# Silu in one ScalarE step, and the place of the MLP norm's sums of squares

## The chip, the cores and the metric

The kernel runs on one core of a Trainium2 chip. The time is the device time of one execution in microseconds; a comparison uses the median of several executions. The engines are named as the profile names them: PE is the matrix engine (PEld its weight loads), DVE the vector engine, ACT the scalar engine, POOL GpSimd, SP the queue that issues nearly all DMAs. Each engine works through its own list of instructions in order; semaphores tie the lists together.

## The reference

Two decoder layers over 512 tokens and 1024 features, in fp32. Cut to what the change touches:

```python
z = h @ w_in                       # split into attention q k v, retention q k v g, two gates
r = chunkwise_retention(rq, rk, rv)
r = r * lax.rsqrt(jnp.mean(r * r, axis=-1, keepdims=True) + EPS)
r = r.reshape(B, S, RET_V) * jax.nn.silu(rg.astype(jnp.float32))
...
h2 = rmsnorm(x, g_mlp)
x = x + jnp.square(jax.nn.relu(h2 @ w_up)) @ w_down
```

`rg` has 1024 columns, eight chunks of 128. `rmsnorm` divides each token by the root of the mean of its squares.

## The kernel before

Activations lie feature-major: eight chunks of 128 features by 512 tokens. Every fp32 factor is split into a high and a low part in a reduced format, and a product is three matmuls, high by high, high by low, low by high (`products`, L332 to L334). Weights arrive in units of 128 x 1024 (SP's DMAs into `raw`); ACT rounds a unit to its high half (L286) and DVE subtracts for the low half (L287). `raw`, `hi` and `lo` have three buffers each, taken in turn, and `unit` splits up to two units ahead of the one in use, so the high half of a unit goes into the buffer of the unit three before.

A layer runs through `w_in` (with attention and retention put between its matmuls as background steps), `w_a`, `w_b`, `w_out` and the MLP. Parts of `w_b`, `w_out` and `w_up` are done as pairs of chunks by a scheme with seven half-size products instead of eight (`narrow_pair` with 256-wide matmuls, `wide_pair` with 512-wide ones for the high weights). A pair uses four pieces of weights and three PSUM banks, called a, b and e. Its first product goes into a, ACT copies a into b (L640), the second product goes into e, and the third adds to b. Later ACT copies the finished b and e into SBUF (L643, L647).

The gates of retention: `put_rg` multiplies a chunk by the token factor on DVE (L970), and `silu` (L976) makes Sigmoid on ACT (L978) and the product with it on DVE (L979). The first four chunks get it after the attention, near the Sigmoid of the other gates (L1124); the last four as they come, while the second half of the retention and the chunks of gate b (`gate`, L904, Sigmoid) run. ACT holds one table of functions at a time; a step whose function is not in the table is preceded by a table load.

The MLP norm: `Rms.prepare` splits the sum over the chunks of x squared into two parts, sh and sl; `Rms.finish` calls `inverse_rms_halved` (L457): two matmuls with a matrix of ones (ssq), two square roots on ACT (L465), a reciprocal on DVE (L466), and four copies on ACT (L469) that lay out rstd. The norm is applied after the matmul, when the products leave PSUM: `put_up` (L1313) for the first four chunks of the MLP, `positive` for the pair behind them. These first four chunks are one `group` (L387): four PSUM banks at once, four units of weights, each unit with two halves (j = 0, 1) of twelve matmuls. A hook after unit 0 calls `prepare`, a hook after unit 1 calls `finish`. Then come the pairs (0, 2), narrow, and (0, 3), wide; the evacuations of the four chunks are put between the steps of the pair.

What sets the order: the program is traced once, in the order of the Python code, and the framework's scheduler then orders each engine's list by its own estimate of times (`schedule_with_timeline_sim=True`). A later call can therefore come earlier in an engine's list. `tc.issue_after(ins)` pins what is traced inside it behind `ins` on the engine of `ins`.

Of the kernel before, what the change touches and what calls it, by code (L numbers as in the profile page):

```python
# [2 lines left out]

# [10 lines left out]
AF = mybir.ActivationFunctionType  # L14
ALU = mybir.AluOpType
# [3 lines left out]
P = 128  # L19
T = 512  # L20
D = 1024
KD = D // P
# [59 lines left out]
def mlp_sequence():  # L82

    seq = [("first", 0, 0), ("pair", 0, 2), ("pair", 0, 3)]
    for q in range(3):
        for i in range(4):
            seq += [("down", q, i), ("pair", q + 1, i)]
    return seq + [("last", 3, 0)]  # L90
# [37 lines left out]
def decoder(ctx, tc, xT, x_first, w_in, w_a, w_b, w_out, w_up, w_down, tables, decay, band, triangles, g_last, out):  # L128
    nc = tc.nc
# [13 lines left out]
    def temp(name="t"):  # L143
        return tmp.tile([P, T], F32, tag="t", name=name)

    def big(name, dtype=F32):
        return tmp.tile([P, 2, T], dtype, tag="big", name=name, bufs=7)

    def bank(pool, name):
        return pool.tile([P, T], F32, tag=pool.name, name=name)  # L150
# [141 lines left out]
    def unit(name, layer):  # L292
        i = state["next"]
        assert order[i][:2] == (layer, name), (order[i], layer, name)
        state["next"] += 1
        split_until(i + 3)
        return parts.pop(i)
# [7 lines left out]
    ones = const.tile([P, P], F32R, name="ones")  # L305
# [20 lines left out]
    def products(ps, pairs, start, stop, resume=False):  # L326


        n = len(pairs)
        for i, ((ah, al), (bh, bl)) in enumerate(pairs):  # L330
            more = {"skip_group_check": True} if resume else {}
            nc.tensor.matmul(ps, ah, bh, start=start and i == 0, stop=False, **more)  # L332
            nc.tensor.matmul(ps, ah, bl, start=False, stop=False, **more)  # L333
            nc.tensor.matmul(ps, al, bh, start=False, stop=stop and i == n - 1, **more)  # L334

    def split(hi, lo, src, scale=None):

        if scale is None:
            nc.scalar.activation(hi, src, AF.Copy)  # L339
            nc.vector.tensor_tensor(lo, src, f32(hi), ALU.subtract)  # L340
        else:
            nc.scalar.activation(hi, src, AF.Copy, scale=scale)  # L342
            nc.vector.scalar_tensor_tensor(lo, src, scale, f32(hi), ALU.mult, ALU.subtract)

    xs, x_homes = [], []
# [6 lines left out]
    def old_input():  # L352
        for t in x_homes:
            slots.give(*t[1])
# [29 lines left out]
        products(ps, pairs[n // 2 :], False, True)  # L384
        evacuate(ps)

    def group(name, layer, moving, evacuates, meanwhile=None):  # L387


        banks = [bank(ps_mm, "mm") for _ in range(4)]  # L390
        for u in range(4):
            hi, lo = unit(name, layer)
            for j in range(2):
                k = 2 * u + j
                for c, ps in enumerate(banks):
                    cols = slice(j * T + c * P, j * T + (c + 1) * P)
                    products(ps, [((hi[:, cols], lo[:, cols]), moving[k])], k == 0, k == KD - 1)
            if meanwhile and u in meanwhile:
                meanwhile[u]()
        return [partial(evacuate, ps) for ps, evacuate in zip(banks, evacuates)]  # L400

    def all_of(steps):
        for step in steps:
            step()
# [52 lines left out]
    def inverse_rms_halved(both, n, dest):  # L457

        ps = bank(ps_aux, "ssq")
        for i, part in enumerate(both):  # L460
            nc.tensor.matmul(ps, ones, part, start=i == 0, stop=i == len(both) - 1)
        own = temp("own")[:, : T // 2]
        sides = [(slice(a * P // 2, (a + 1) * P // 2), slice(a * T // 2, (a + 1) * T // 2)) for a in range(2)]
        for rows, cols in sides:
            nc.scalar.activation(own[rows, :], ps[rows, cols], AF.Sqrt, bias=eps[rows, :], scale=1.0 / n)  # L465
        nc.vector.reciprocal(own, own)  # L466
        for rows, cols in sides:
            for there, _ in sides:
                nc.scalar.activation(dest[there, cols], own[rows, :], AF.Copy)  # L469

    def inverse_rms(both, n, dest):

        ps = bank(ps_aux, "ssq")
        for i, part in enumerate(both):
            nc.tensor.matmul(ps, ones, part, start=i == 0, stop=i == len(both) - 1)
        nc.scalar.activation(dest, ps, AF.Sqrt, bias=eps, scale=1.0 / n)
        nc.vector.reciprocal(dest, dest)
# [12 lines left out]
    class Rms:  # L490
# [7 lines left out]

        def finish(self):
            self.value = tmp.tile([P, T], F32, tag="rstd", name="rstd", bufs=2)  # L500
            (inverse_rms if self.folded else inverse_rms_halved)(self.parts, D, self.value)


    def end(layer, uT):
# [76 lines left out]
    def layer_body(layer):  # L581
        g_mix, g_mlp = 2 * layer, 2 * layer + 1
        rms_mix, rms_mlp = Rms(g_mix, True), Rms(g_mlp, False)
# [10 lines left out]
        def sum_input(by_form, b, ks):  # L594

            (b11, b12), (b21, b22) = ((t[:, :, :H], t[:, :, H:]) for t in b)
            f = [big("sums").rearrange("p a (b t) -> p (a b) t", t=H) for _ in range(2)]
            t1, t2, t3, t4 = f[0][:, 0:2, :], f[0][:, 2:4, :], f[1][:, 0:2, :], f[1][:, 2:4, :]

            def parts_of_forms(j):  # L600
                t = by_form[2 * (j // 2) + ks // 2]
                return [t[:, :, :, s, :] for s in range(2)]

            nc.vector.tensor_tensor(t1, b12, b11, ALU.subtract)
            nc.vector.tensor_tensor(t2, b22, t1, ALU.subtract)
            split(*parts_of_forms(0), f[0].rearrange("p (j k) t -> p j k t", k=2))
            nc.vector.tensor_tensor(t3, b22, b12, ALU.subtract)
            nc.vector.tensor_tensor(t4, b21, t2, ALU.subtract)
            split(*parts_of_forms(2), f[1].rearrange("p (j k) t -> p j k t", k=2))

        def scaled_pair(ks, which):

            b = [big("xg") for _ in range(2)]
            for part, g in ((0, ks), (1, ks + 4)):
                for i in range(2):
                    col = which * KD + g + i
                    nc.scalar.activation(b[part][:, i, :], x[:, g + i, :], AF.Copy, scale=gain[:, col : col + 1])
            return b
# [342 lines left out]
        rg, rg_next, rg_tiles = {}, {}, {}  # L961
# [12 lines left out]
            return put  # L974

        def silu(i):  # L976
            s = temp("sig")
            nc.scalar.activation(s, rg[i], AF.Sigmoid)  # L978
            nc.vector.tensor_tensor(rg[i], rg[i], s, ALU.mult)  # L979

        ret = {}

# [156 lines left out]
        for u in range(4):  # L1139
            hi, lo = unit("w_a", layer)  # L1140
            for j in range(2):
                c = 2 * u + j
                ps = bank(ps_mm, "mm")
                pairs = []
                for k in range(4):
                    cols = slice(k * 256 + j * P, k * 256 + (j + 1) * P)
# [158 lines left out]
        by_form = [h[1] for h in homes_x]  # L1305
# [108 lines left out]
        def put_down(c, last=False):  # L1414
            def put(ps):
                nc.vector.tensor_tensor(x[:, c, :], x[:, c, :], ps, ALU.add)  # L1416
                if last:
                    scaled_input(c, g_mix + 2)
                    squared_input(c, g_mix + 2)
                    nc.sync.dma_start(spill[:, c, :], x[:, c, :])  # L1420

            return put

        def first_hooks():
            def at1():
                rms_mlp.finish()
                sum_input(by_form, scaled_pair(2, g_mlp), 2)

            return {0: lambda: (rms_mlp.prepare(), sum_input(by_form, scaled_pair(0, g_mlp), 0)), 1: at1}

        for what, q, i in mlp_sequence():
            if what == "first":
                late = group("w_up", layer, xs, [put_up] * 4, first_hooks())
            elif what == "pair":
                pair(q, i, late)
                if (q, i) == (3, 3):
                    old_input()
                    for t, _ in homes_x:
                        slots.give(*t[1])
            elif what == "down":  # L1440
                two_chunks("w_down", layer, up[q], [put_down(2 * i), put_down(2 * i + 1)])
                if i == 3:
                    slots.give(*up_slots[q])
            elif layer == DEPTH - 1:
                end(layer, up[q])
            else:
                new_input()
                all_of(group("w_down", layer, up[q], [put_down(c, True) for c in range(4)]))
                for c in range(4, KD):
                    chunk("w_down", layer, up[q], put_down(c, True))  # L1450
                slots.give(*up_slots[q])
# [10 lines left out]
    for layer in range(DEPTH):  # L1462
        layer_body(layer)
# [175 lines left out]
```

## Time and profile before

| what | value |
|---|---|
| median of 3 runs | 1472.45 us (1472.3 to 1472.51) |
| profiled execution | 1473.8 us |
| its span, first to last instruction | 1472.0 us |
| granted PE clock | 0.999 |
| PE busy | 1464.8 us (100%), 7466 matmuls |
| DVE busy | 1166.7 us (79%) |
| ACT busy | 810.9 us (55%) |

A row of the timeline reads: start in us from the span's start, duration, engine, line of the kernel, operation, output<-inputs, shape, count; in brackets the idle time of the engine ahead of it and what ended it. A row of the groups reads: line, engine, operation, count, then busy us and mean ns of one, then idle us ahead and what ended it. PE's matmuls overlap, so the distance of two starts, and not the duration, is what a matmul costs.

### The profile page before, as it was taken

The numbers are of one execution on the slowest core, as the hardware profiler recorded it, in microseconds if no ns is written. First come the engines' busy times: TensorE is split into PE (matmuls) and PEld (weight loads), VectorE is DVE, ScalarE is ACT, GpSimd is POOL, SyncE is SP. The second block draws the span as 40 slices with busy tenths as digits, with TensorE's granted clock in tenths as the row PEclk, the third lists the DMA queues.
The fourth block names the chain that finished last, engine by engine and source line by source line (L and its number), as shares of the span: only waits on it lengthen the run. The fifth ranks groups of instructions, "written<-read, shape, count | busy, mean of one in ns | idle before, by whom it ended". The sixth has DMA issues, their size and how long they took to land.

```text
span 1472.0 us, 20220 instructions
## 1 busy us (share of the span) xinstructions
PE 1464.8 (100%) x7466; PEld 1249.6 (85%) x7466; DVE 1166.7 (79%) x1920; ACT 810.9 (55%) x1306; POOL 3.8 (0%) x14
## 2 busy tenths in 40 slices
PE   9999999999999999999999999999999999999998
PEld 7888888888988888888888888888989888888887
DVE  7998878778988787776678986786899877878763
ACT  7656356654684445444455753656547754444553
POOL 0000000000000000000000000000000000000000
PEclk9999999999999999999999999999999999999999
DMA  6422843356443332333543258333654522333241
GB/s 227 127 89 92 300 158 99 102 172 212 126 126 118 101 115 93 104 104 115 165 126 97 86 186 272 104 104 102 207 171 126 154 95 93 114 106 109 90 140 57
DMA packets 71043, 194.45 MB, mean 132 GB/s; under 512 B 8457, under 2 KB 8609, under 8 KB 70945
## 3 DMA queue, kind: packets, MB, share of 16 engines
q1 hardware_dynamic: 70656, 192.65, 40.7%
q8 instruction: 58, 0.95, 0.3%
q10 hardware_dynamic: 288, 0.52, 0.1%
q14 instruction: 41, 0.33, 0.1%
HBM read 171.63 MB, written 18.89 MB: 129 GB/s over the span
## 4 chain that ended last, share of the span: by engine, by line
PE 94%; issue 5%; DMA 1%; DVE 0%; ACT 0%; POOLq 0%; DVEq 0%; SPq 0%
PE mm L334 22%; PE mm L332 22%; PE mm L333 22%; PE mm L1336 11%; PE mm L1337 5%; PE rv L332 2%; PE rv L333 2%; PE rv L334 2%; PE score L842 1%; PE r L332 1%; PE r L334 1%; PE r L333 1%; PE pT L797 0%; PE pv L823 0%; PE pv L824 0%
## 5 line engine op out<-in xcount | busy, mean ns | idle before, releaser
L333 PE MATMUL mm<-r,hi 128*128 128x512 f32 (+1 forms) x1568 | 572.5, 367 | 0.0
L332 PE MATMUL mm<-r,hi 128*128 128x512 f32 (+1 forms) x1568 | 569.7, 367 | 0.6 <-ACT r L342 0.6
L334 PE MATMUL mm<-r,lo 128*128 128x512 f32 (+1 forms) x1568 | 563.9, 367 | 0.2
L286 ACT ACTIVATE hi<-raw 128x1024 fp32r<-128x1024 f32 (+1 forms) x334 | 334.1, 1002 | 386.4 <-PE mm L333 206.8
L287 DVE TENSOR_TENSOR lo<-raw,hi 128x512 fp32r<-128x512 f32 (+1 forms) x335 | 384.7, 1151 | 111.6 <-ACT hi L286 107.9
L334 PEld LDWEIGHTS mm<-r,lo 128*128 128x128 f32 x1568 | 293.7, 188 | 48.7 <-DVE lo L287 1.4
L332 PEld LDWEIGHTS mm<-r,hi 128*128 128x128 f32 x1568 | 293.8, 188 | 47.5 <-ACT r L342 1.4
L333 PEld LDWEIGHTS mm<-r,hi 128*128 128x128 f32 x1568 | 294.3, 188 | 45.9
L1336 PE MATMUL mm<-r,hi 128*128 128x512 f32 x728 | 252.1, 391 | 0.0
L1337 PE MATMUL mm<-r,lo 128*128 128x256 f32 x728 | 200.5, 277 | 0.0
L1336 PEld LDWEIGHTS mm<-r,hi 128*128 128x128 f32 x728 | 136.5, 188 | 28.6
L1337 PEld LDWEIGHTS mm<-r,lo 128*128 128x128 f32 x728 | 136.7, 188 | 3.1 <-DVE lo L287 0.7
L1416 DVE TENSOR_TENSOR x<-x,mm 128x512 f32<-128x512 f32 x56 | 37.8, 686 | 28.9 <-PE mm L334 28.9
L1409 ACT ACTIVATE z<-z 128x512 f32<-128x512 f32 x56 | 32.4, 623 | 48.7 <-DVE z L1389 48.7
L333 PE MATMUL rv<-lo,r 128*128 128x512 f32 x128 | 49.8, 389 | 0.0
L334 PE MATMUL rv<-hi,r 128*128 128x512 f32 x128 | 49.5, 389 | 0.0
L332 PE MATMUL rv<-hi,r 128*128 128x512 f32 x128 | 49.4, 390 | 0.0
L340 DVE TENSOR_TENSOR r<-z,r 128x512 fp32r<-128x512 f32 x64 | 42.9, 686 | 3.0 <-ACT r L339 2.6
L339 ACT ACTIVATE r<-z 128x512 fp32r<-128x512 f32 x64 | 38.4, 619 | 7.9 <-DVE z L1070 7.8
L869 ACT ACTIVATE sm<-sm,st 128x256 f32<-128x256 f32 (+1 forms) x64 | 30.1, 472 | 18.9 <-DVE st L857 18.7
L1389 DVE SCALAR_TENSOR_TENSOR z<-z,rstd 128x512 f32<-128x512 f32 x52 | 35.7, 687 | 0.6
L340 DVE TENSOR_TENSOR r<-sums,r 128x1024 fp32r<-128x1024 f32 x24 | 28.9, 1220 | 0.0
(273 smaller groups left out, 1693.0 us busy)
## 6 DMA issues: line engine op xcount, KB each, us to landing
raw<-w_in_in SPq DMA_DIRECT2D x89, 512.0 KB, 3.7
raw<-w_down_in SPq DMA_DIRECT2D x64, 512.0 KB, 3.6
raw<-w_up_in SPq DMA_DIRECT2D x32, 512.0 KB, 4.0
raw<-w_up_in SPq DMA_DIRECT2D x60, 256.0 KB, 2.9
raw<-w_a_in SPq DMA_DIRECT2D x8, 512.0 KB, 4.8
ahead<-w_b_in SPq DMA_DIRECT2D x8, 512.0 KB, 5.4
park_w_b<-ahead SPq DMA_DIRECT2D x16, 256.0 KB, 5.7
ahead<-w_up_in SPq DMA_DIRECT2D x8, 512.0 KB, 4.9
```

Source lines behind the costliest of these rows:

```text
L286: nc.scalar.activation(hi[:, at], raw[:, at], AF.Copy)
L287: last_low[:] = [nc.vector.tensor_tensor(lo[:, at], raw[:, at], f32(hi[:, at]), ALU.subtract).ins]
L332: nc.tensor.matmul(ps, ah, bh, start=start and i == 0, stop=False, **more)
L333: nc.tensor.matmul(ps, ah, bl, start=False, stop=False, **more)
L334: nc.tensor.matmul(ps, al, bh, start=False, stop=stop and i == n - 1, **more)
L339: nc.scalar.activation(hi, src, AF.Copy)
L340: nc.vector.tensor_tensor(lo, src, f32(hi), ALU.subtract)
L1336: nc.tensor.matmul(both, hi[:, c], m, start=start and k == 0, stop=False, **more)
L1337: nc.tensor.matmul(ps[:, :H], lo[:, c], m[:, 0, :], start=False, stop=k == 3 and start, **more)
L1389: nc.vector.scalar_tensor_tensor(z[:, :, at], z[:, :, at], 0.0, factor, ALU.max, ALU.mult)
L1409: nc.scalar.activation(z[:, i, :], z[:, i, :], AF.Square)
L1416: nc.vector.tensor_tensor(x[:, c, :], x[:, c, :], ps, ALU.add)
```

## The change

`silu` becomes one ACT step with the Silu function, in place. The call of `rms_mlp.finish` leaves the hook after unit 1. `group` gets an argument `between`: ahead of the second half of its last unit it is called, and that half's matmuls are pinned behind the last of the two ssq matmuls on PE. `inverse_rms_halved` and `Rms.finish` return that matmul.

```diff
-    def group(name, layer, moving, evacuates, meanwhile=None):
+    def group(name, layer, moving, evacuates, meanwhile=None, between=None):
...
                 k = 2 * u + j
-                for c, ps in enumerate(banks):
-                    cols = slice(j * T + c * P, j * T + (c + 1) * P)
-                    products(ps, [((hi[:, cols], lo[:, cols]), moving[k])], k == 0, k == KD - 1)
+                with tc.issue_after(between()) if between and (u, j) == (3, 1) else nullcontext():
+                    for c, ps in enumerate(banks):
+                        cols = slice(j * T + c * P, j * T + (c + 1) * P)
+                        products(ps, [((hi[:, cols], lo[:, cols]), moving[k])], k == 0, k == KD - 1)
...
-            nc.tensor.matmul(ps, ones, part, start=i == 0, stop=i == len(both) - 1)
+            summed = nc.tensor.matmul(ps, ones, part, start=i == 0, stop=i == len(both) - 1).ins
...
+        return summed
...
-            (inverse_rms if self.folded else inverse_rms_halved)(self.parts, D, self.value)
+            return (inverse_rms if self.folded else inverse_rms_halved)(self.parts, D, self.value)
...
         def silu(i):
-            s = temp("sig")
-            nc.scalar.activation(s, rg[i], AF.Sigmoid)
-            nc.vector.tensor_tensor(rg[i], rg[i], s, ALU.mult)
+            nc.scalar.activation(rg[i], rg[i], AF.Silu)
...
-            def at1():
-                rms_mlp.finish()
-                sum_input(by_form, scaled_pair(2, g_mlp), 2)
+            def at0():
+                rms_mlp.prepare()
+                sum_input(by_form, scaled_pair(0, g_mlp), 0)
 
-            return {0: lambda: (rms_mlp.prepare(), sum_input(by_form, scaled_pair(0, g_mlp), 0)), 1: at1}
+            return {0: at0, 1: lambda: sum_input(by_form, scaled_pair(2, g_mlp), 2)}
...
-                late = group("w_up", layer, xs, [put_up] * 4, first_hooks())
+                late = group("w_up", layer, xs, [put_up] * 4, first_hooks(), rms_mlp.finish)
```

More of the change, by code (lines that the diff above doesn't have):

```diff
@@ L1 @@
 from contextlib import ExitStack
+from contextlib import nullcontext
 from functools import partial
```

## The prediction

> **What bounds the kernel now.** I read the page first (span, busy time, chain), then the list of who waited for whom on PE and on its weight loads, then the timeline of the two places that the edits touch.
>
> ```profile
> span 1472.0 us, 20220 instructions
> ...
> PE 1464.8 (100%) x7466; PEld 1249.6 (85%) x7466; DVE 1166.7 (79%) x1920; ACT 810.9 (55%) x1306; POOL 3.8 (0%) x14
> ...
> PE 94%; issue 5%; DMA 1%; DVE 0%; ACT 0%; POOLq 0%; DVEq 0%; SPq 0%
> ```
>
> PE is busy from end to end and the chain of work that ended last is nearly all PE. A change that leaves the 7466 matmuls alone can only take away waits of PE, or add some. The list of waits (in all, times, longest) says how much there is to take:
>
> ```profile
> PE warm L311 <- DVE ones L306: 1.0, 1, 1.0
> PEld mm L334 <- DVE lo L287: 1.4, 6, 0.3
> PEld mm L1337 <- DVE lo L287: 0.7, 2, 0.3
> ```
>
> Beside the start-up, PE's weight loads wait for low halves that DVE brings late, 2.1 us in all. That is 0.14% of the span and the most that these edits could win. I count 0.2% (2.94 us) as about what a measurement of this kernel can tell from no change, so a gain beyond it is all but excluded. The question is which new waits arise.
>
> **The sums below** are differences, made against the profiled execution (1473.8 us; its span is 1472.0). The median of the unprofiled runs is 1472.45, 1.35 lower; I add the differences to that median.
>
> **Edit 1, silu in one step.** Per layer eight Sigmoids and eight products leave, eight Silus come. The groups (count, then busy and mean ns of one, then idle before) and two stretches (PE, PEld, DVE, ACT busy us of the stretch) of the gates of layer 0:
>
> ```profile
> L979 DVE TENSOR_TENSOR z<-z,sig 128x512 f32<-128x512 f32 x16 | 10.7, 686 | 3.5 <-ACT sig L978 3.5
> L978 ACT ACTIVATE sig<-z 128x512 f32<-128x512 f32 x16 | 9.6, 622 | 0.1
> L978 ACT ACT_TABLE_LOAD x2 | 2.6, 1283 | 0.2 <-DVE z L970 0.2
> ```
> ```profile
> 120.00:160.00 40.00, 40.00 (x182) 33.12 (x181) 34.67 (x63) 23.87 (x31) 0.00 (x0) 1.00 0.45 143
> 240.00:330.00 90.00, 90.00 (x460) 77.26 (x459) 70.87 (x104) 53.97 (x79) 0.00 (x0) 1.00 0.40 127
> ```
> ```profile
> L286 ACT ACTIVATE hi<-raw 128x1024 fp32r<-128x1024 f32 (+1 forms) x35 | 36.5, 1044 | 43.4 <-PE mm L333 33.1 <-issue 5.3 <-PE rv L334 4.5
> ```
>
> DVE loses 16 x 0.686 = 11.0 us of work. No Silu is in this trace; I price it as the Sigmoid of the same tile, 0.62 us, so ACT's arithmetic stays. Silu is not in Sigmoid's table: the changed program has 23 table loads where this one has 19, two more per layer. One stands ahead of the first four Silus (behind the Sigmoid of the other gates, in the first stretch), one ahead of the Sigmoids that follow the last four (in the second). A load costs what these two rows show, load and next step 1.30 us apart:
>
> ```profile
> 253.90 1.28 ACT L978 ACT_TABLE_LOAD   x1 [0.17 <-DVE z L970]
> 255.20 0.63 ACT L978 ACTIVATE sig<-z 128x512 f32<-128x512 f32 x1
> ```
>
> So ACT gains 4 x 1.30 = 5.2 us and DVE loses 11.0. What does PE see of it? In both stretches PE is busy throughout, so nothing is there to win. ACT is busy 24 of 40 and 54 of 90 us. Its weight splits between 120 and 330 us (the last row of the groups) stood idle for 43.4 us, 33.1 of them because PE had not yet freed the buffer: ACT runs ahead of PE and catches up 1.3 us within one or two units. I take 0 for edit 1; the cover is that head start. Bounds: 0 below, since PE has no idle time here to give back; 5.2 us above, if all four loads fell on PE's path. Zero is nearer, by the 33.1.
>
> The page "ScalarE: Activation LUTs" of the Trainium skill, section "What ACT_TABLE_LOAD costs", speaks against this edit: it asks for about 1.28 us of load plus 1.38 of drain, 2.66 a switch. By it ACT would gain an estimated 10.6 us, still hidden, or 10.6 on the path at worst. The trace has the load but no drain behind it (1.30 from row to row), so the trace decides.
>
> **Edit 2, the squares between the halves.** The "first" group multiplies four chunks in four units (512-wide), then the pair behind it runs in four pieces (256-wide products; I call its banks a, b, e as the code does). Before, the two ssq products stood inside the last unit; PE in layer 0, then ACT, then DVE:
>
> ```profile
> 418.06 0.39 PE L333 MATMUL mm<-r,hi 128*128 128x512 f32 x1
> ...
> 420.77 0.39 PE L461 MATMUL ssq<-sh,ones 128*128 128x512 f32 x1
> 421.00 0.39 PE L333 MATMUL mm<-r,hi 128*128 128x512 f32 x1
> ...
> 423.72 0.39 PE L461 MATMUL ssq<-sl,ones 128*128 128x512 f32 x1
> ...
> 424.40 0.28 PE L332 MATMUL mm<-r,hi 128*128 128x256 f32 x1
> ...
> 425.81 0.28 PE L332 MATMUL mm<-r,hi 128*128 128x256 f32 x1
> ...
> 427.23 0.28 PE L332 MATMUL mm<-r,hi 128*128 128x256 f32 x1
> ```
> ```profile
> 418.53 1.06 ACT L286 ACTIVATE hi<-raw 128x1024 fp32r<-128x1024 f32 x1 [2.01 <-PE mm L333]
> 419.50 1.04 ACT L339 ACTIVATE r<-sums 128x1024 fp32r<-128x1024 f32 x1
> 420.56 1.28 ACT L465 ACT_TABLE_LOAD   x1
> 424.15 0.95 ACT L465 ACTIVATE own<-ssq,x 64x256 f32<-64x256 f32 x2 [2.31 <-PE ssq L461]
> 425.12 1.06 ACT L286 ACTIVATE hi<-raw 128x1024 fp32r<-128x1024 f32 x1
> 426.21 0.37 ACT L640 ACTIVATE mm<-mm 128x256 f32<-128x256 f32 x1
> 426.92 1.70 ACT L469 ACTIVATE rstd<-own 64x256 f32<-64x256 f32 x4 [0.34 <-DVE own L466]
> 428.64 0.63 ACT L286 ACTIVATE hi<-raw 128x512 fp32r<-128x512 f32 x1
> ```
> ```profile
> 419.63 1.23 DVE L287 TENSOR_TENSOR lo<-raw,hi 128x1024 fp32r<-128x1024 f32 x1
> ...
> 425.13 1.75 DVE L466 RECIPROCAL own<-own 128x256 f32<-128x256 f32 x1 [3.14 <-ACT own L465]
> ```
>
> A 512-wide product takes 0.227 us of PE (420.77 to 421.00), a 256-wide one 0.118 (twelve from 424.40 to 425.81). In the changed program PE's order is: the rest of the first half (two products), ssq<-sh, ten of the pair's twelve products into a, ssq<-sl, all twelve products of the second half, the last two into a, then e and b as before. So:
> - ssq<-sh at 420.77 + 2 x 0.227 = 421.22. The ten moved ahead need piece 0's low half at about 421.7; it is there at 419.63 + 1.23 = 420.86. No wait.
> - ssq<-sl at 421.22 + 0.23 + 10 x 0.118 = 422.63, which is 1.09 earlier. ACT's square roots start 0.43 behind it (423.72 to 424.15), at 423.06, and end at 424.01; the reciprocal ends at 424.04 + 1.75 = 425.79.
> - The second half runs from 422.86; its last product with the high weights is the eleventh, at 422.86 + 10 x 0.227 = 425.13. PE's sum of work is the same, so e is due at 425.81 and the next b at 427.23, unchanged.
>
> The catch is ACT's order. Behind the square roots comes, as before, the high half of the pair's piece 2. There are three weight buffers, and this half goes where unit 3, the last of the group, still lies. ACT follows the freeing product by 0.47 us (418.06 to 418.53), so it starts at 425.13 + 0.47 = 425.60, with ACT standing idle from 424.01. Behind it now stand the four rstd copies and only then the copy of a into b (L640, L643 after); before, that copy stood ahead of them. So: high half 425.60, rstd 0.97 later (418.53 to 419.50) at 426.57, the copy 1.72 later (426.92 to 428.64) at 428.29, done at 428.66, seen by PE at about 428.71. PE's product into b is due at 427.23, and behind it in PE's queue stands all the rest. **New stall: 1.48 us per layer.** Before, the copy was done at 426.58, 0.65 early. The norm itself hardly gains: rstd done 428.29, against 428.62.
>
> **What comes back.** The wide pair behind it waits in both layers, for its low half:
>
> ```profile
> 430.91 1.04 ACT L286 ACTIVATE hi<-raw 128x1024 fp32r<-128x1024 f32 x1
> ```
> ```profile
> 432.01 1.22 DVE L287 TENSOR_TENSOR lo<-raw,hi 128x1024 fp32r<-128x1024 f32 x1
> ```
> ```profile
> 432.88 0.40 PE L1336 MATMUL mm<-r,hi 128*128 128x512 f32 x1
> 433.28 0.39 PE L1337 MATMUL mm<-r,lo 128*128 128x256 f32 x1
> 433.51 0.40 PE L1336 MATMUL mm<-r,hi 128*128 128x512 f32 x1
> ```
>
> The first two steps take 0.40 and 0.23 instead of 0.23 and 0.12: 0.28 us lost. After, PE wants that low half at 432.88 + 0.23 + 1.48 = 434.59. Its high half waits for piece 1's buffer, freed about 1.48 later than now, so it starts near 431.8, ends near 432.8, and the low half near 434.1. That is half a microsecond early; the 0.28 goes.
>
> **Sum.** Edit 1: 0. Edit 2: 2 layers x (1.48 - 0.28) = +2.4. 1472.45 + 2.4 = 1474.85, that is +0.16%, inside the 0.2%. Bounds for the stall: 0 below (ACT gets its buffer without waiting); above, 1.48 with nothing given back and a second wait, as below.
>
> **Rivals.**
> - A shorter stall. If piece 2's high half is not held by unit 3 (its buffer free by 424.0), rstd waits for the reciprocal alone, 425.82, and the copy is done at 425.82 + 1.72 + 0.37 = 427.91: 0.73 of stall remain, less 0.28, so 1472.45 + 2 x 0.45 = 1473.35. If the copy also got ahead of rstd, as it stood before, there is no stall and the 0.28 is won: 1472.45 - 0.56 = 1471.9, the other side. For it: ssq really ends 1.09 earlier. Against it: the wait at 418.53, the same buffer rule one unit before, and the order of the changed program.
> - Slower. The copy of the finished b out of its bank (L647) falls behind the first chunk's square and split (0.63 each) in ACT's new order, and PE may not add to b before it. I work it out as done near 431.0 and due at 428.71 + 24 x 0.118 = 431.5. If DVE brings the chunk late, PE stalls again. Two ACT steps are 1.26, less the 0.5 in hand: up to 0.8, say 0.6 a layer: 1474.85 + 1.2 = 1476.05. It decides (beyond 2.94) from 0.27 a layer on. For it: DVE sits behind the reciprocal until 425.8; against it, DVE has nothing ahead of that chunk but one low half, 1.2 us.
> - The table loads reach PE, through a score split or a gate late on ACT: half of the 5.2 would give 1474.85 + 2.6 = 1477.5. Against it stands the head start above.
>
> **Chances.** The forecast (0.9 to 1.5 net a layer) 0.57; the shorter stall 0.10 and the full gain 0.03; the second stall 0.23; the table loads 0.05; anything else 0.02. Of the forecast's own 0.57 (1474.2 to 1475.4) I put 0.04 beyond 2.94. So slower 0.04 + 0.23 + 0.05 + 0.01 = 0.33, faster 0.01, same 0.66. Range 1472.4 to 1476.3: it takes in the shorter stall, the forecast and the second stall and leaves out the full gain and the table loads.
>
> **What would show it.** Right: in the list of waits PE's product into b waits on ACT's mm copy about 1.5 us, twice; ACT's high half right behind the square roots shows an idle of about 1.6 released by PE; the wait of the wide pair for DVE lo is gone; 23 table loads and no PE wait in the gates. Wrong: the copy ends before 427.3; or a wait on ACT's eu copies; or PE waits between 130 and 320 us.

## The result, and the profile after

| | before | after |
|---|---|---|
| median of 17 runs each | 1472.67 us | 1475.39 us |
| ratio | | 1.0019, 95% interval 1.0012 to 1.0027 |
| profiled execution | 1473.8 us | 1475.36 us |
| span | 1472.0 us | 1473.6 us |

The changed kernel is 2.72 us slower, 0.19%: the interval excludes no change, and the difference is still within the 0.2%, though the upper end of the interval, 0.27%, is not. The two profiled executions differ by less, 1.6 us, because in the one of before the first columns of x came about 1.2 us later than in the one of after (the first step on them starts at 5.53 against 4.30). So every time in the trace of after is 1.1 to 1.2 us earlier than the same event in the trace of before, up to the place where the kernels part.

The page of after, then its list of waits of PE and PEld (in all, times, longest):

```profile
span 1473.6 us, 20199 instructions
...
PE 1464.4 (99%) x7466; PEld 1249.4 (85%) x7466; DVE 1157.6 (79%) x1904; ACT 817.3 (55%) x1310; POOL 3.8 (0%) x14
...
PE 93%; issue 5%; ACT 0%; DVE 0%; DMA 0%; POOLq 0%; DVEq 0%; SPq 0%
```
```profile
PEld mm L333 <- ACT mm L643: 3.0, 2, 1.5
...
PE mm L333 <- ACT mm L643: 2.6, 2, 1.3
...
PEld mm L335 <- DVE lo L288: 1.2, 5, 0.3
...
PEld mm L1337 <- ACT bu L1371: 0.4, 2, 0.2
```

Line numbers are 1 to 3 higher than before (L640 is now L643). The first two rows are new: two waits, one a layer, for ACT's copy of a into b. The two waits of the wide pair for DVE's low half (before: PEld mm L1337 <- DVE lo, 0.7) are gone, and in the last row there is a smaller one that before did not have, for bu. (eu and bu are ACT's copies of finished banks into SBUF; in the wide pair bu is that of b.)

The stretch itself in layer 0, ACT, then DVE, then PE:

```profile
421.89 0.95 ACT L467 ACTIVATE own<-ssq,x 64x256 f32<-64x256 f32 x2 [1.23 <-PE ssq L463]
424.48 1.06 ACT L287 ACTIVATE hi<-raw 128x1024 fp32r<-128x1024 f32 x1 [1.64 <-issue]
425.44 1.68 ACT L471 ACTIVATE rstd<-own 64x256 f32<-64x256 f32 x4
427.15 0.37 ACT L643 ACTIVATE mm<-mm 128x256 f32<-128x256 f32 x1
```
```profile
422.87 1.75 DVE L468 RECIPROCAL own<-own 128x256 f32<-128x256 f32 x1 [2.07 <-ACT own L467]
...
431.67 1.23 DVE L288 TENSOR_TENSOR lo<-raw,hi 128x1024 fp32r<-128x1024 f32 x1 [0.55 <-ACT hi L287]
```
```profile
424.00 0.39 PE L334 MATMUL mm<-r,hi 128*128 128x512 f32 x1
...
425.98 0.28 PE L335 MATMUL mm<-r,lo 128*128 128x256 f32 x1
427.57 0.39 PE L333 MATMUL mm<-r,hi 128*128 128x256 f32 x1 [1.30 <-ACT mm L643]
427.79 0.28 PE L334 MATMUL mm<-r,hi 128*128 128x256 f32 x1
```

Read it from the bottom. PE's last product into e starts at 425.98; the next, the first into b, would follow 0.118 later, at 426.10, and starts at 427.57: 1.47 us lost. ACT's copy ends at 427.15 + 0.37 = 427.52. ACT had stood idle for 1.64 us, from 422.84 to 424.48, ahead of the high half of piece 2, which starts 0.48 behind the product at 424.00. The profile calls this idle "issue", not a wait for PE. The copy's own input had been ready since about 424.9, when the last product into a was through.

In the tables below, "lost PE time" is worked out from the trace: for each matmul the distance to the next start, less the usual distance of its shape (0.227 us for a 512-wide, 0.118 for a 256-wide product), summed over a stretch. Over the MLP's first 145 us it is 0.72 us in layer 0 and 0.49 in layer 1 before, 2.03 and 1.97 after: +2.79 us in all, beside the measured +2.72. The level of these figures hangs on the last digit of the two distances (with exactly 0.227 and 0.118 every stretch comes out some 0.24 lower); the differences between kernels do not.

### The profile page after: what moved, and what is told of

It reads as the page before. It is cut to its first block, busy times and chain, and to the rows that moved or that the text cites. A ratio compares the mean times of both kernels' runs of the same rounds, so it can differ in the third digit from the quotient of the medians.

```text
span 1473.6 us, 20199 instructions
## 1 busy us (share of the span) xinstructions
PE 1464.4 (99%) x7466; PEld 1249.4 (85%) x7466; DVE 1157.6 (79%) x1904; ACT 817.3 (55%) x1310; POOL 3.8 (0%) x14
## 4 chain that ended last, share of the span: by engine, by line
PE 93%; issue 5%; ACT 0%; DVE 0%; DMA 0%; POOLq 0%; DVEq 0%; SPq 0%
PE mm L333 22%; PE mm L335 22%; PE mm L334 22%; PE mm L1337 11%; PE mm L1338 5%; PE rv L333 2%; PE rv L335 2%; PE rv L334 2%; PE score L845 1%; PE r L333 1%; PE r L335 1%; PE r L334 1%; PE pT L800 0%; PE pv L826 0%; PE pv L827 0%
## 5 line engine op out<-in xcount | busy, mean ns | idle before, releaser
L334 PE MATMUL mm<-r,hi 128*128 128x512 f32 (+1 forms) x1568 | 572.5, 367 | 0.0
L334 PEld LDWEIGHTS mm<-r,hi 128*128 128x128 f32 x1568 | 294.3, 188 | 46.2
L1337 PE MATMUL mm<-r,hi 128*128 128x512 f32 x728 | 252.2, 391 | 0.0
L1337 PEld LDWEIGHTS mm<-r,hi 128*128 128x128 f32 x728 | 136.5, 188 | 29.1 <-ACT bu L1371 0.4
L334 PE MATMUL rv<-lo,r 128*128 128x512 f32 x128 | 49.8, 389 | 0.0
```

Of the source, the lines that this page charges most:

```text
L1337: nc.tensor.matmul(both, hi[:, c], m, start=start and k == 0, stop=False, **more)
```

## The experiments

Each was timed beside runs of the kernel before on the same chip; "to before" is the difference of the medians. One interval is about 1.3 us to either side, so what decides between theories is mostly the waits in the trace, with the medians as a check on their sum.

| kernel | to before, us | ratio, 95% interval | lost PE time in the MLP stretches, layer 0 + 1 | to before |
|---|---|---|---|---|
| before | | | 0.72 + 0.49 | |
| after | +2.72 | 1.0012 to 1.0027 | 2.03 + 1.97 | +2.79 |
| edit 1 alone | -0.60 | 0.9987 to 1.0005 | 0.51 + 0.46 | -0.25 |
| the same again | -0.64 | 0.9988 to 1.0006 | 0.49 + 0.46 | -0.27 |
| edit 2 alone | +3.40 | 1.0014 to 1.0032 | 2.06 + 2.01 | +2.85 |
| before, ACT's order alone | +4.00 | 1.0015 to 1.0034 | 2.65 + 2.35 | +3.78 |
| after, rstd behind the copy | +0.45 | 0.9992 to 1.0010 | 1.12 + 0.62 | +0.52 |
| after, copy on DVE | +0.63 | 0.9994 to 1.0012 | 1.21 + 0.71 | +0.70 |
| after, piece 2 split later | +1.87 | 1.0001 to 1.0019 | 1.66 + 1.10 | +1.55 |
| after, squares ahead of the unit | +0.53 | 0.9994 to 1.0012 | 0.96 + 0.68 | +0.43 |
| edit 1 and 20 more table loads | +2.08 | 1.0004 to 1.0022 | 0.50 + 0.48 | -0.24 |
| edit 1, first split behind the weights | +0.47 | 0.9994 to 1.0012 | 0.98 + 0.63 | +0.39 |

### Which of the two edits

Edit 1 alone: the kernel before with

```diff
         def silu(i):
-            s = temp("sig")
-            nc.scalar.activation(s, rg[i], AF.Sigmoid)
-            nc.vector.tensor_tensor(rg[i], rg[i], s, ALU.mult)
+            nc.scalar.activation(rg[i], rg[i], AF.Silu)
```

> The kernel before with only edit 1: silu in one ACT step; the sums of squares stay where they were. Theory: the four added table loads (5.2 us of ACT) are hidden; PE's list of waits is that of the kernel before (DVE lo about 2.1 us in all), ACT's copy of a into b ends ahead of its due time, and the time is that of the kernel before, difference 0 (-0.3 to +0.3 us). Rival, the table loads reach PE: +0.5 to +5.2 us, with PE waits on ACT between 130 and 320 us of the span or the same stretch of layer 1.

Measured -0.60 us, below the -0.3 that I gave, and PE waits for nothing in the gates. A Silu of 128x512 is as long as the Sigmoid was, and a load still takes 1.28 (edit 1 alone, ACT):

```profile
252.63 1.28 ACT L977 ACT_TABLE_LOAD   x1
253.93 0.63 ACT L977 ACTIVATE z<-z 128x512 f32<-128x512 f32 x1
```

Since the trace explained 0.25 at most, the same kernel was run a second time.

> The kernel before with edit 1 alone, a second time, because the first time it came out 0.6 us below the kernel before while the waits in its trace explain 0.1 or less. If that was the scatter of the start-up: -0.3 to +0.3 us this time. If edit 1 really gains: -0.4 to -0.8 us again.

-0.64 again. Each interval holds 0, but the two medians agree. The lost PE time of the first 15 us is 2.3 and 2.2 us in these two traces and 3.1 in that of before; it is 1.9 to 2.9 in the other traces, though what the engines do there is the same instructions. Behind the first 15 us, and outside the MLP stretches, PE's times in these two traces and in that of before differ by less than 0.1 us in all. So the half microsecond may belong to the start-up, where PE waits for the first x, rather than to the gates. Of the twelve traces, the three of kernels without edit 1 lose 3.1, 2.9 and 2.3 there and the nine with it 1.9 to 2.8; one trace of each kernel is too little to say that edit 1 does it. No run settles it.

Edit 2 alone: the changed kernel with those three lines of `silu` put back.

> The changed kernel with edit 1 undone: Sigmoid and a product again, the sums of squares between the halves. Theory: the whole difference is here: +2.7 us to the kernel before (2.4 to 3.0), PE's product into b waits on ACT's copy for about 1.47 us of PE time in each layer, and there are 19 table loads. Rival, part of the difference is the table loads: clearly less than the changed kernel, +2.2 us or below.

+3.40, and these are its waits for the copy, the same as those of after:

```profile
PEld mm L333 <- ACT mm L643: 3.0, 2, 1.5
...
PE mm L333 <- ACT mm L643: 2.6, 2, 1.3
```

The whole loss is edit 2's. The median is above the 2.4 to 3.0 that I gave; the trace (+2.85) is inside it. The two edits add up: -0.60 + 3.40 = 2.80, measured together 2.72. But the medians of both lie off their traces by about half a microsecond (-0.60 against -0.25, +3.40 against +2.85), in opposite directions; in the other rows of the table whose waits lie in the MLP stretches the median lies 0.07 below to 0.32 above the trace. So what the medians say to a few tenths is not explained by the waits.

### Is it ACT's order?

The kernel before, with nothing but this copy pinned behind the last of the four rstd copies:

```diff
             for there, _ in sides:
-                nc.scalar.activation(dest[there, cols], own[rows, :], AF.Copy)
+                last_lay[:] = [nc.scalar.activation(dest[there, cols], own[rows, :], AF.Copy).ins]
...
-            ins = nc.scalar.activation(b, a, AF.Copy).ins
+            with tc.issue_after(last_lay.pop()) if last_lay else nullcontext():
+                ins = nc.scalar.activation(b, a, AF.Copy).ins
```

> The kernel before with ACT's order alone changed: the copy of a into b is pinned behind the four rstd copies; no Silu, the sums of squares stay in their late place. Theory: the order makes the stall; the rstd copies end at 428.6, the copy at 429.0, due at 427.23: 1.8 us of stall a layer, less up to 0.28 given back: +3.0 to +3.9 us to the kernel before, so more than the changed kernel. Rival (the place of the sums on PE makes the stall): 0 us.

+4.00 us, a little above the 3.0 to 3.9 that I gave. Its ACT, then PE:

```profile
426.37 1.70 ACT L470 ACTIVATE rstd<-own 64x256 f32<-64x256 f32 x4 [0.74 <-DVE own L467]
428.09 0.37 ACT L643 ACTIVATE mm<-mm 128x256 f32<-128x256 f32 x1
```
```profile
426.56 0.28 PE L335 MATMUL mm<-r,lo 128*128 128x256 f32 x1
428.51 0.38 PE L333 MATMUL mm<-r,hi 128*128 128x256 f32 x1 [1.67 <-ACT mm L643]
```

Due at 426.56 + 0.118 = 426.68, started at 428.51: 1.83 us lost, as worked out; waits of 0.1 to 0.3 us in the pairs behind, which I had not counted, add to it. The order of two items on ACT costs more than the whole change did, with the squares in their old place. In the changed kernel the earlier squares take back only 0.36 of it (1.83 to 1.47).

The counterpart is the changed kernel with the copy ahead of rstd again. `inverse_rms_halved` keeps its four copies for later, and the pair's first step issues them:

```diff
-        for rows, cols in sides:
-            for there, _ in sides:
-                nc.scalar.activation(dest[there, cols], own[rows, :], AF.Copy)
+        def lay_out():
+            for rows, cols in sides:
+                for there, _ in sides:
+                    nc.scalar.activation(dest[there, cols], own[rows, :], AF.Copy)
+
+        laid.append(lay_out)
...
             def step(ins):
                 now = next(turn)
+                while laid:
+                    with tc.issue_after(ins):
+                        laid.pop()()
```

> The changed kernel with the four rstd copies pinned behind the copy of a into b on ACT: the order that the kernel before has, but with the sums of squares 1.09 us earlier. Theory: ACT takes the high half about 425.6, then the copy, done by about 427.0 on the trace of the kernel before, 0.2 ahead of its due time; no stall, the 0.28 a layer of the wide pair's wait is back, rstd is no earlier than in the kernel before: 0 us to the kernel before (-0.6 to +0.4). Rival, the stall comes from the high half that waits for unit 3's buffer and not from the order: +1 us or more.

Its ACT, and the wait that is left in the wide pair:

```profile
424.44 1.06 ACT L287 ACTIVATE hi<-raw 128x1024 fp32r<-128x1024 f32 x1 [1.64 <-issue]
425.53 0.37 ACT L647 ACTIVATE mm<-mm 128x256 f32<-128x256 f32 x1
425.81 1.69 ACT L472 ACTIVATE rstd<-own 64x256 f32<-64x256 f32 x4
```
```profile
PEld mm L1342 <- DVE lo L288: 0.7, 2, 0.4
```

The 1.64 us of idle and its place are those of the changed kernel, and there is no stall: the copy is done at 425.90, and PE goes through without a gap. The buffer's wait is harmless as long as the copy is the next thing behind it. The wide pair's wait is back, 0.31 a layer. The rest of the +0.52 is waits of 0.1 to 0.35 us in the pairs behind, which I had not counted; the interval holds 0, and the median is just above the -0.6 to +0.4 that I gave.

The third way round the order: the copy of pair (0, 2) on DVE.

```diff
-            ins = nc.scalar.activation(b, a, AF.Copy).ins
+            ins = (nc.vector.tensor_copy(b, a) if on_dve else nc.scalar.activation(b, a, AF.Copy)).ins
...
-            z = ... else narrow_pair(pool, step, form, block, positive)
+            z = ... else narrow_pair(pool, step, form, block, positive, (q, i) == (0, 2))
```

> The changed kernel with one instruction moved: the copy of a into b of the pair (0, 2) runs on DVE, behind the reciprocal, and not on ACT behind the four rstd copies. Theory (what PE waits for is that one copy's place in ACT's order): the copy is done 0.3 us or more ahead of its due time, no stall at b in either layer, and the wide pair's wait for its low half (0.28 a layer) stays or goes with it: 0 to -0.6 us to the kernel before, 2.7 to 3.3 below the changed kernel. Rival, the norm itself is late (rstd, the evacuations and not the copy hold PE): +1.5 to +3 us to the kernel before, with PE waits on eu or on the low half in place of the one on the copy.

Its DVE and its wide pair:

```profile
425.13 0.43 DVE L643 COPY mm<-mm 128x256 f32<-128x256 f32 x1 [0.26 <-PE mm L335]
```
```profile
PEld mm L1338 <- DVE lo L288: 0.9, 2, 0.5
```

The stall at b is gone in both layers, with the norm where the change put it: the norm itself held nobody up. But the size was a miss: +0.63, where I had 0 to -0.6. It is 2.1 us better than the changed kernel (each against its own runs of before) and not 2.7 to 3.3: the wide pair loses 0.42 a layer for its low half instead of 0.28, and in layer 0 another 0.34 comes later.

### How much of it is the buffer

Piece 2 is split one unit later and its high half pinned behind the copy; nothing that waits for unit 3 then stands ahead of rstd:

```diff
-                    nc.scalar.activation(hi[:, at], raw[:, at], AF.Copy)
+                    with tc.issue_after(last_copy[0]) if order[i][1:] == ("pair", 4, 2, "w_up") else nullcontext():
+                        nc.scalar.activation(hi[:, at], raw[:, at], AF.Copy)
...
-        split_until(i + 3)
+        split_until(i + (2 if order[i][1:] == ("pair", 4, 0, "w_up") else 3))
...
             ins = nc.scalar.activation(b, a, AF.Copy).ins
+            last_copy[:] = [ins]
```

> The changed kernel with the high half of the pair's piece 2 behind the copy of a into b on ACT: the wait for unit 3's buffer no longer stands ahead of the rstd copies, but these still stand ahead of the copy. Theory (the stall is the later of two terms: the buffer and the reciprocal): the rstd copies start with the reciprocal's end, and the copy is done about 0.65 to 0.75 us too late for PE instead of 1.47: +0.9 to +1.6 us to the kernel before. Against it, a new wait on the low half of piece 2 could add 0.3 to 1 a layer. Rival (the buffer counts for nothing): the stall stays 1.47 and the time +2.7.

```profile
425.06 1.70 ACT L473 ACTIVATE rstd<-own 64x256 f32<-64x256 f32 x4 [1.82 <-DVE own L470]
426.78 0.37 ACT L645 ACTIVATE mm<-mm 128x256 f32<-128x256 f32 x1
```
```profile
426.39 0.28 PE L337 MATMUL mm<-r,lo 128*128 128x256 f32 x1
427.20 0.39 PE L335 MATMUL mm<-r,hi 128*128 128x256 f32 x1 [0.54 <-ACT mm L645]
```

Now rstd waits for the reciprocal (1.82, DVE own), and PE loses 427.20 - 426.39 - 0.118 = 0.69 us a layer instead of 1.47. So the stall of the change has two parts: 0.69 because the norm's result is needed ahead of the copy, and 0.78 because a weight half ahead of both waits for its buffer. The median, +1.87, is a little above the 0.9 to 1.6; the trace has +1.55, with the new wait (0.36 + 0.11 in layer 0, for eu) that the expectation allowed for.

### The table loads

A Sigmoid of one column, whose result nobody uses, ahead of each Silu, on top of edit 1:

```diff
+            one = small.tile([P, 8], F32, tag="st", name="st")[:, 0:1]
+            nc.scalar.activation(one, rg[i][:, 0:1], AF.Sigmoid)
             nc.scalar.activation(rg[i], rg[i], AF.Silu)
```

> The kernel before with edit 1, and a Sigmoid of one column ahead of every Silu, whose result nobody uses: 20 table loads more than with edit 1 alone, some 26 us on ACT and 20 short steps, in the gates of both layers. It measures how much ACT time the gates can take before PE feels it. Theory (the loads are hidden by ACT's head start): 0 to +3 us to the kernel before. Rival (a load ahead of a Silu delays PE by a good part of its length): +10 to +26 us.

The page's busy times, what PE and PEld newly wait for, and two of the loads on ACT:

```profile
PE 1464.4 (99%) x7466; PEld 1248.4 (85%) x7466; DVE 1156.2 (78%) x1904; ACT 842.9 (57%) x1346; POOL 3.8 (0%) x14
```
```profile
PEld rv L333 <- DVE lo L287: 1.2, 1, 1.2
PE ssq L447 <- DVE sh L340: 1.2, 2, 0.6
```
```profile
253.90 1.28 ACT L978 ACT_TABLE_LOAD   x1
255.19 0.20 ACT L978 ACTIVATE st<-z 128x1 f32<-128x1 f32 x1
255.41 1.28 ACT L979 ACT_TABLE_LOAD   x1
256.71 0.63 ACT L979 ACTIVATE z<-z 128x512 f32<-128x512 f32 x1
```

ACT is busy for 26.5 us more than with edit 1 alone (842.9 against 816.4), and the median is 2.4 to 2.5 us above that of edit 1 alone. Three places give it: one low half of weights about 1 us late (rv, in layer 0), and a sum of squares that is multiplied between the gates (ssq, L447) 0.8 late in each layer. In the table's last column this stands outside the MLP stretches. So 20 loads beyond those of edit 1, with their short steps, bring PE a tenth of their length, and edit 1's four bring nothing that the trace shows. Load and next step are 1.29 and 1.30 us apart here too. The page "ScalarE: Activation LUTs" of the Trainium skill, section "What ACT_TABLE_LOAD costs", adds 1.38 of drain to each switch; in these rows, where loads follow steps within 0.02 us, there is no room for one.

### Two attempts at a better kernel

The squares ahead of the whole last unit, 2.7 us earlier than between its halves:

```diff
-                with tc.issue_after(between()) if between and (u, j) == (3, 1) else nullcontext():
+                with tc.issue_after(between()) if between and (u, j) == (3, 0) else nullcontext():
```

> The changed kernel with the sums of squares ahead of the whole last unit instead of between its halves, 2.7 us earlier still; ACT's list is then copied by the same scheduler. Theory: the reciprocal ends while ACT still waits for nothing, the rstd copies stand ahead of the high half that is held by unit 3's buffer, and the copy of a into b is on time: no stall at b; with the evacuations earlier the wide pair's wait goes too: -0.6 to 0 us to the kernel before. Rival (any earlier place of the sums delays the pair): +1 us or more.

```profile
423.30 1.70 ACT L471 ACTIVATE rstd<-own 64x256 f32<-64x256 f32 x4 [1.82 <-DVE own L468]
425.03 1.58 ACT L287 ACTIVATE hi<-raw 128x1024 fp32r<-128x1024 f32 x2
```
```profile
PEld mm L1337 <- ACT bu L1371: 0.9, 2, 0.5
```

The copy now comes ahead of the square roots in ACT's list (418.87 against 420.53), rstd runs in the time in which ACT would wait for unit 3, and neither the stall at b nor the wide pair's wait for its low half is left. But bu in the wide pair, 0.2 late in the changed kernel, is 0.5 late, and in layer 0 another low half costs 0.33: no gain, +0.53, where I had given -0.6 to 0.

Edit 1 with the first chunk's split held back behind the weights that the wide pair waits for:

```diff
-            split(view(hi), view(lo), t)
+            if up[0]:
+                split(view(hi), view(lo), t)
+            else:
+                waiting.append(lambda: split(view(hi), view(lo), t))
...
                 now = next(turn)
+                while now == 4 and waiting:
+                    with tc.issue_after(last_high[0]), tc.issue_after(last_low[0]):
+                        waiting.pop()()
```

> The kernel before with edit 1, and the split of the first MLP chunk (ACT's high half, DVE's low half) pinned behind that of the first weight unit of the wide pair, which the wide pair waits for 0.28 us in both layers. Theory: ACT takes the weight unit's high half 0.5 us earlier, the low half is there in time, and both waits are gone: 0.56 us less than with edit 1 alone, so -0.6 to -1.2 us to the kernel before. Rival (the chunk's split is what is late next): a new wait of 0.2 to 0.5 us a layer elsewhere in the pair, no gain.

```profile
PEld mm L334 <- DVE lo L287: 1.9, 6, 0.5
...
PEld mm L1337 <- ACT bu L1371: 0.6, 2, 0.3
```

The rival held: PE's 0.28 for the weights went in both layers, and waits for bu (0.24 a layer) and for another low half (up to 0.45; PEld mm L334 had 1.4 in all before) came in its place. Neither beats the kernel before; the lowest median is that of edit 1 alone, and its interval does not separate it from the kernel before.

## Why the prediction was right, point by point

- **Edit 1 costs nothing on PE.** Held: four loads more (the rows of after below: 6 and 4, where before has 4 and 2), no wait in the gates, and the median is not above that of before. The cover is larger than I showed: 26.5 us of extra ACT work gave 2.5. The 0.6 below zero was outside my bounds; it is measured twice, not separated from 0, and not explained.

```profile
L907 ACT ACT_TABLE_LOAD x6 | 7.7, 1283 | 0.1
L980 ACT ACT_TABLE_LOAD x4 | 5.1, 1283 | 0.1
```

- **The stall, 1.48 a layer.** Measured 1.47 in both. Each link stands in the trace of after, 1.12 to 1.17 earlier than I put it, which is the start-up's difference: square roots 421.89 (forecast 423.06), high half 424.48 (425.60), rstd 425.44 (426.57), copy done 427.52 (428.66), PE on at 427.57 (428.71).
- **What holds the high half.** I said the buffer of unit 3, and the idle would be shown as released by PE. The idle is there, 1.64, but the profile names no releaser. That it is the buffer follows from the 0.48 behind the freeing product, and from the run that takes this half out of the way: the stall falls by 0.78 to 0.69, where my "shorter stall" had 0.73.
- **The order, not the place of the squares.** The prediction made the copy's place behind rstd the cause. The kernel before with that order alone loses 1.83; the changed kernel with the old order, or with the copy on DVE, loses nothing there. The page "Perfetto Trace Analysis" of the Trainium skill, section "Tensor Engine Instruction (MATMUL, LD_WEIGHTS)", says that ACT and DVE take their instructions strictly first in, first out; the rows of after agree, with ACT idle for 1.64 us ahead of one step and the copy still to come 2.3 us after its input was ready, at about 424.9.
- **What comes back, 0.28.** Held: the low half is done at 431.67 + 1.23 = 432.90, and PE wants it at 433.56, behind the first product of the wide pair.

```profile
433.33 0.40 PE L1337 MATMUL mm<-r,hi 128*128 128x512 f32 x1
```

- **The sum, where the size was off.** I had 1.48 - 0.28 = 1.20 a layer. Two terms were missing: behind the stall the second product starts 0.225 later and not 0.118 (427.57 to 427.79), 0.11 more, and the new wait for bu costs another 0.11. 1.47 + 0.11 + 0.11 - 0.28 = 1.41, two layers 2.8; the trace has 2.79, the median 2.72. That the median agrees so well is partly luck: edit 2 alone, with the same stalls, came out at +3.40, and the -0.6 of edit 1, for which this sum has no term, brings it back. The forecast time, 1474.85, was 0.54 below the measured one: 0.32 by the difference (2.4 against 2.72) and 0.22 by the median of before, 1472.45 in three runs and 1472.67 in seventeen. The first of the two I could have read off: in the rows of before, too, the product behind a wait takes twice its usual distance, and in the 0.28 I had counted exactly that.
- **The second stall (rival).** Did not come: the copy of b out of its bank, which I put at 431.0, is in time, and PE waits for no eu. The list of waits has nothing from it. The small new wait is for bu, one pair further on.
- **A row misread.** The low half at 419.63 that I quoted as piece 0's is piece 1's. Piece 0's is the row below, from the trace of before, done at 417.17; the step "no wait" stands.

```profile
415.94 1.23 DVE L287 TENSOR_TENSOR lo<-raw,hi 128x1024 fp32r<-128x1024 f32 x1
```

## What to carry to other kernels

When a result is made earlier, look at what its consumers push back on the engine that they share with something urgent: here the sums of squares came 1.1 us earlier and rstd 0.36, and the price was a copy that PE needed, now last behind a step held by a buffer and four that nobody was in a hurry for. List that engine's order in both programs, give each item the time at which its input is there and the time at which its output is wanted, and the stall comes out to a few hundredths of a microsecond. Here, with PE busy for 99%, a removed wait of 0.3 us mostly came back as one or two others in the next pairs, so a new order is only worth trying if it shortens something that PE waits for by more than that.

## What was not expected

- The start-up differs from trace to trace. The lost PE time of the first 15 us is between 1.9 and 3.1 us over twelve traces in which the work of that stretch is the same; a difference between two kernels of under 1 us cannot be read from two profiled spans.
- A wait of PE cost about 0.11 us more than the wait itself: behind each stall at b the second product started 0.22 to 0.23 us behind the first instead of 0.118, after 0.69 us of waiting as after 1.83. With 512-wide products it was about the same 0.11: 0.33 instead of 0.227 behind the late low half (rv) of the run with 20 more table loads.
- 20 table loads of 1.28 us reached PE with about 2.5 us in all.
